# Half-step FFNs of a hybrid decoder layer: hidden blocks that `down` takes plainly without their sums, another order of the second pair's sums, and other ways for the first P6 weights, the first norm's gain and the last weights of `down`

## The chip, the cores and the metric

The kernel runs on one core of one Trainium2 chip. The metric is device time of one launch in microseconds; the time of the kernel before is the median of three runs. One further execution was taken by the hardware profiler, and every row below is from that one. In the rows PE is TensorE (matmuls and transposes; PEld its weight loads), DVE is VectorE, ACT ScalarE, POOL GpSimd, SP SyncE. SPq and ACTq are the DMA issues of SP and ACT.

## The reference

One layer of a hybrid decoder for 1040 prompt positions (16 learned tokens and 1024) and 64 sample positions: a half-step FFN, a token mixer (gated delta rule beside sliding-window attention), and a second half-step FFN. The change lies in the FFNs and in what comes just before each.

```python
def rms_norm(x, g):
    xf = x.astype(jnp.float32)
    y = xf * lax.rsqrt(jnp.mean(xf * xf, axis=-1, keepdims=True) + RMS_EPS)
    return (y * g.astype(jnp.float32)).astype(x.dtype)

def swiglu(x, w_gate, w_up, w_down):
    return (jax.nn.silu(x @ w_gate) * (x @ w_up)) @ w_down

def half_ffn(h, g_pre, g_post, w_gate, w_up, w_down):
    return h + 0.5 * rms_norm(swiglu(rms_norm(h, g_pre), w_gate, w_up, w_down), g_post)
```

`D_MODEL` is 1024, `D_FF` 2816, and all is float32.

## The kernel before, in words

Each FFN is one object of class `Ffn` (lines 168 to 577). It multiplies by one level of the Strassen-Winograd scheme: tokens (1104 in FFN1, 1088 in FFN2), model width and hidden width are each halved, and seven products P1 to P7 of half-size blocks take the place of eight. The sums and differences of token blocks are the `x1` to `x7` tiles (`left` makes x1 and x2 of a tile of 128 tokens, `right` the other five, from two tiles and with transposes on TensorE, `place`, line 206). Those of weight blocks are `T` (`difference`, line 254, on VectorE). Every operand is split into a high part, cast on ACT (`wh` line 278, `x..h` line 208, `hs` line 370) and a low part, the rest, subtracted on POOL for weights (`wl` line 279) and on VectorE otherwise (`x..l` line 209, `hs` line 358). A product is three matmuls per step, high by high, low by high, high by low (`FAST`). One product of a pair has 24 pairs of matmuls in gate and up and goes to PSUM bank A, B or C (line 305).

The hidden width is handled in 11 pairs f = 0 to 10 of 128 columns from each half. The order of a pair is gate (kind g), then up (kind u); `start` runs P1 and P2 of the first two pairs while the tokens come in (`weave` puts pieces of two generators into the program in turn, here matmuls and `tiles_in` for FFN1, `Merge.rest` for FFN2), then `ea1`, the pools of that phase, are closed, others opened, and `up(2)` runs the rest: P6, P5, P7, P4, P3 for the first two pairs and P1, P6, P5, P7, P2, P4, P3 for the others, each for g and u. The adds that take a bank away are on VectorE: `u2` after P6 (line 343), `s` after P7 and, on the same P7 plus bank C, `u3` (line 346), then after P4 and P3. P4 goes to a B bank (two of them), which the add after P6 sets free; P3 is added on top of P5 in bank C, which `u3` has read first.

When a pair is done, `hidden(f)` multiplies gate by up and makes the seven operand blocks that the products of `down` need. Blocks 1, 4, 8 and 2 are the plain ones, 5, 6, 7 and 3 are sums and differences of them, `S1` and `S2` hold them. `split` makes both parts, and `store` writes them to DRAM (`hid`) from ACT's queue, the last pair's, f = 10, mostly from SP's (line 376). It is a generator: `self.late` is advanced one step after each product of the following pair but P6, and what is left is drained at the end of `up`.

`down` goes over groups of pairs (0, 1), (2, 3, 4), (5, 6), (7, 8), (9, 10). For each of the seven products of a group it loads the blocks (`hb`, from SP's queue, line 458) and multiplies them by split weight blocks into accumulators (line 473); the first group copies its products to the accumulators on ACT (line 512), in the order P1, P2, P3, P6, P5, P7, P4. The last group, f = 9 and 10, is `plain`: it uses the four ordinary products with weights 11, 21, 12 and 22 and reads blocks 1, 2, 8 and 4 alone. Its weights lie in two pools, `wp` (that of the groups before) and `wp2`. VectorE and POOL add accumulators to one another meanwhile (`beside`).

The framework orders the instructions of each engine by its own estimate of time, and the waits between engines are semaphores; an instruction waits at the head of its engine's queue, a DMA issue as well.

## Time and profile before

| | |
|---|---|
| median of 3 runs | 2802.1 us (2795.24 to 2806.37) |
| the profiled execution's own time | 2796.77 us |
| its span | 2795.0 us |
| TensorE busy | 2669.6 us, 96% |
| VectorE, ACT, POOL busy | 1619.9, 1099.8, 1390.0 us |
| mean granted TensorE clock | 0.979 |
| DMA | 413.88 MB, 148 GB/s over the span |

FFN1 ends near 760 us, the mixer near 1950, FFN2 at the end. The chain of work that ended last is TensorE nearly all along. A wait of TensorE is a row "engine line waited for: us in total, times, longest us". In a window's row stand the stretch, its length, busy us of the engine (with the number of instructions), the granted clock (1.00 is full), the DMA engines' share and GB/s.

### The profile page before, as it was taken

To read this page: it belongs to the slowest core of one execution; us is meant where nothing else is said; L and a number is where in the kernel's file an instruction comes from. 1 tells how busy PE (TensorE), PEld (TensorE's weight loads), DVE (VectorE), ACT (ScalarE), POOL (GpSimd) and SP (SyncE) were. 2 spreads that over 40 slices of the span, in tenths; PEclk is the share of its full clock that TensorE was granted. 3 is DMA by queue.
4 is the path that set the end of the run, shared out by engine and by line. 5 is a ranking of instruction groups with operands and counts; after the bars stand their busy time and mean duration, and the time that the engine had idled before them with its cause. 6 is when DMAs were issued, how large, how long until landed. Compare 5 with 4: busy or idle time off the path is not lost. (4 is left out here: it accounts for less than half of the span.)

```text
span 2795.0 us, 49454 instructions
## 1 busy us (share of the span) xinstructions
PE 2669.6 (96%) x18957; PEld 2502.6 (90%) x18957; DVE 1619.9 (58%) x2415; ACT 1099.8 (39%) x2592; POOL 1390.0 (50%) x1296
## 2 busy tenths in 40 slices
PE   7999999899978999999999999998999999999998
PEld 6999999899977898788788888887789999999997
DVE  7757566446546659954444444443557556555575
ACT  5333333322155632354444444444443334343221
POOL 5655555445446644644434443444455555554471
PEclk9999999999988999999999999999999999999998
DMA  4344343677433653354333333334434344348763
GB/s 154 130 150 159 122 151 143 246 237 239 168 121 113 212 180 96 99 170 116 100 88 95 94 92 95 92 92 138 136 125 157 118 153 162 118 151 325 240 224 122
DMA packets 230994, 413.88 MB, mean 148 GB/s; under 512 B 59894, under 2 KB 121494, under 8 KB 230470
## 3 DMA queue, kind: packets, MB, share of 16 engines
q1 hardware_dynamic: 209302, 327.67, 36.5%
q10 hardware_dynamic: 21456, 83.05, 7.4%
q8 instruction: 150, 2.46, 0.4%
q14 instruction: 86, 0.70, 0.1%
HBM read 262.78 MB, written 149.51 MB: 148 GB/s over the span
## 5 line engine op out<-in xcount | busy, mean ns | idle before, releaser
L132 PE MATMUL gu<-xh,wl 128*128 128x512 f32 (+3 forms) x1456 | 502.8, 345 | 0.1
L279 POOL TENSOR_TENSOR wl<-T,wh 128x512 fp32r<-128x512 f32 x248 | 338.3, 1370 | 326.7 <-ACT wh L278 237.0
L128 PE MATMUL gu<-xh,wh 128*128 128x512 f32 (+3 forms) x1456 | 498.5, 342 | 0.0
L130 PE MATMUL gu<-xl,wh 128*128 128x512 f32 (+3 forms) x1456 | 497.4, 342 | 0.0
L473 PE MATMUL y<-hb,wh 128*128 128x256 f32 (+2 forms) x2528 | 434.7, 292 | 15.8 <-DMA hb<-hid 9.7
L279 POOL TENSOR_TENSOR wl<-raw,wh 128x512 fp32r<-128x512 f32 x198 | 272.5, 1382 | 267.3 <-ACT wh L278 220.5
L473 PEld LDWEIGHTS y<-hb,wh 128*128 128x128 f32 x2528 | 370.1, 190 | 18.1 <-DMA hb<-hid 10.5
L132 PEld LDWEIGHTS gu<-xh,wl 128*128 128x128 f32 x1456 | 281.6, 193 | 28.8 <-issue 11.1
L130 PEld LDWEIGHTS gu<-xl,wh 128*128 128x128 f32 x1456 | 281.9, 194 | 19.9 <-issue 1.2
L128 PEld LDWEIGHTS gu<-xh,wh 128*128 128x128 f32 x1456 | 281.8, 194 | 18.6 <-issue 1.6
L278 ACT CAST wh<-T 128x512 fp32r<-128x512 f32 x248 | 153.3, 621 | 349.0 <-PE B L305 109.0
L473 PE MATMUL y<-hb,wl 128*128 128x256 f32 (+2 forms) x1264 | 274.5, 291 | 5.5 <-POOL wl L279 5.5
L278 ACT CAST wh<-raw 128x512 fp32r<-128x512 f32 x198 | 122.1, 620 | 288.5 <-PE y L473 103.5
L484 DVE TENSOR_TENSOR acc<-acc,y 128x552 f32<-128x552 f32 (+4 forms) x216 | 144.9, 679 | 154.3 <-PE y L473 153.8
L752 POOL TENSOR_TENSOR wl<-raw,wh 128x1024 fp32r<-128x1024 f32 x60 | 145.4, 2424 | 143.5 <-ACT wh L751 121.1
L473 PEld LDWEIGHTS y<-hb,wl 128*128 128x128 f32 x1264 | 208.9, 190 | 6.8 <-POOL wl L279 6.7
L254 DVE TENSOR_TENSOR T<-raw,raw 128x512 f32<-128x512 f32 x124 | 118.7, 960 | 105.5 <-POOL wl L279 102.6
L1514 POOL TENSOR_TENSOR f<-f,mhalf 128x1 f32<-128x1 f32 (+1 forms) x72 | 54.6, 759 | 113.1 <-DVE f L1512 107.5
L264 DVE TENSOR_TENSOR T<-raw,T 128x512 f32<-128x512 f32 x62 | 70.9, 1146 | 67.9 <-POOL wl L279 67.8
L905 DVE SCALAR_TENSOR_TENSOR cv<-pc,cw,cv 128x1131 f32<-128x1131 f32 x48 | 75.1, 1567 | 34.2 <-POOL cv L902 33.8
L254 DVE TENSOR_TENSOR T<-raw,T 128x512 f32<-128x512 f32 x62 | 65.6, 1064 | 32.1 <-POOL wl L279 31.9
L370 ACT CAST hs<-S 128x552 fp32r<-128x552 f32 (+1 forms) x60 | 39.1, 652 | 111.3 <-DVE S L358 68.1
(585 smaller groups left out, 7489.0 us busy)
## 6 DMA issues: line engine op xcount, KB each, us to landing
hid<-hs ACTq DMA_DIRECT2D x73, 552.0 KB
hid<-hs ACTq DMA_DIRECT2D x73, 544.0 KB
hb<-hid SPq DMA_DIRECT2D x71, 552.0 KB
hb<-hid SPq DMA_DIRECT2D x71, 544.0 KB
raw<-in_w_in_dram SPq DMA_DIRECT2D x58, 512.0 KB
raw<-in_ffn_w_gate_dram SPq DMA_DIRECT2D x94, 256.0 KB
raw<-in_ffn_w_up_dram SPq DMA_DIRECT2D x94, 256.0 KB
raw<-in_ffn_w_down_dram SPq DMA_DIRECT2D x88, 256.0 KB
```

The source lines that it names most:

```text
L128: nc.tensor.matmul(ps, wh, xh, start=first and i == 0, stop=False)
L130: nc.tensor.matmul(ps, wh, xl, start=False, stop=False)
L132: nc.tensor.matmul(ps, wl, xh, start=False, stop=last and i == n - 1)
L254: self.nc.vector.tensor_tensor(out=b[name], in0=b[x], in1=b[y], op=ALU.subtract)
L264: nc.vector.tensor_tensor(out=s, in0=b["21"], in1=s, op=ALU.subtract)
L278: self.nc.scalar.copy(hi, s)
L279: self.nc.gpsimd.tensor_tensor(out=lo, in0=s, in1=f32(hi), op=ALU.subtract)
L473: self.nc.tensor.matmul(self.view(ps[d], (i,)), w[x][:, d * P:(d + 1) * P], hb[:, y, lo:hi], start=j + x + y == 0, stop=j == len(items) - ...
L484: dve = lambda out, x, y: nc.vector.tensor_tensor(out=out, in0=x, in1=y, op=ALU.add)
L752: nc.gpsimd.tensor_tensor(out=lo, in0=raw, in1=f32(hi), op=ALU.subtract)
L905: nc.vector.scalar_tensor_tensor(out=cv, in0=pc[:, w:w + PADW], scalar=self.cw[:, j, w:w + 1], in1=cv, op0=ALU.mult, op1=ALU.add)
L1514: nc.gpsimd.tensor_tensor(out=f[rows], in0=f[rows], in1=c.mhalf[rows, 0:1], op=ALU.pow)
```

## The change

- `hidden`: for f = 9 and 10 only blocks 1, 4, 8 and 2 are made and stored; 5, 6, 7 and 3 and the sums for them are not. That is sixteen stores fewer in the two FFNs.
- `hidden`, other pairs: blocks come in the order 1, 4, 5, 2, 6, 7, 3 (before 1, 4, 5, 6, 2, 7, 3). Both sums are made in the step of block 5, and h12 - S2 is written to S1 in the step of block 2.
- `up`: the steps of `hidden(0)` that follow P7 and P4 of pair 1's gate are issued after the add of P6.
- `sixth_ahead` (new): called before `ea1` closes, it loads blocks 11, 12 and 22 of the first pair's gate weights, makes T2 and splits it, so that the first P6's weights are made there. `w_op` makes T1 and T2 for P4 itself where they are not there.
- `down`, last group: weights 11 and 21 are split into `wp2`, 12 and 22 into `wp`.
- `tiles_in`: the first norm's gain, 1024 values that all partitions need, is loaded as one row from ACT's queue and spread by two matmuls with a row of ones and two copies on VectorE. Norms 2 and 3 are put between the steps of `left(1)`, and their operations keep program order.
- The weaves of `start` with `tiles_in` and `rest` begin at 0.25 of the matmuls (0 and 0.1 before).

```diff
+    def sixth_ahead(self):
+        b, = self.raw("g", (0,), ("11", "12", "22"))
+        t = self.c.t(self.rawp, [P, 512], tag="raw")
+        for out, x, y in ((t, b["12"], b["11"]), (b["22"], b["22"], t)):
+            self.nc.vector.tensor_tensor(out=out, in0=x, in1=y, op=ALU.subtract)
+        self.ready[0, "g", 6] = self.w_split(self.wp, b["22"])
...
             if len(parts) == 2 and p != 6:
-                next(self.late, None)
+                with self.c.tc.issue_after(self.sixth) if p in (7, 4) and (f, kind) == self.begun else nullcontext():
+                    next(self.late, None)
...
         h12 = times("u2")
+        if f in self.plain:
+            split(8, h21)
+            yield
+            store()
+            split(2, h12)
+            yield
+            store()
+            yield
+            return
         s1, s2 = self.v("S1"), self.v("S2")
         op(s1, h21, h22, ALU.add)
+        op(s2, s1, h11, ALU.subtract)
         split(5, s1)
-        yield
-        store()
-        op(s2, s1, h11, ALU.subtract)
-        split(6, s2)
         yield
         store()
         split(2, h12)
-        if f in self.plain:
-            split(8, h21)
+        op(s1, h12, s2, ALU.subtract)
+        yield
+        store()
+        split(6, s2)
+        yield
+        store()
         op(h21, h11, h21, ALU.subtract)
+        split(7, h21)
         yield
         store()
-        split(7, h21)
-        op(s2, h12, s2, ALU.subtract)
-        yield
-        store()
-        split(3, s2)
+        split(3, s1)
...
-        w = {name: [self.w_split(self.wp if name[1] == "1" else self.wp2, x[name]) for x in b]
+        w = {name: [self.w_split(self.wp2 if name[1] == "1" else self.wp, x[name]) for x in b]
...
-                    gain("ffn1_norm_pre", xin)
+                    row, one = c.t(xin, [1, D], tag="row", bufs=1), c.t(xin, [1, P], tag="one", bufs=1)
+                    nc.scalar.dma_start(row, I["ffn1_norm_pre"])
+                    nc.gpsimd.memset(one, 1.0)
+                    g = gains["ffn1_norm_pre"] = c.t(xin, [P, D], tag="g", bufs=1)
+                    for k in range(0, D, 512):
+                        ps = c.t(ptr, [P, 4, P], tag="tr").rearrange("p k t -> p (k t)")
+                        nc.tensor.matmul(ps, one, row[:, k:k + 512], start=True, stop=True)
+                        nc.vector.tensor_copy(g[:, k:k + 512], ps)
...
-                if t in order[:5]:
+                if j == 1:
+                    yield from steps_of(g := f1.left(ptr, xs[t], t), 1)
+                    next(g)
+                    norm(2, c.tc.keep_in_program_order)
+                    norm(3, c.tc.keep_in_program_order)
+                    yield
+                elif t in order[:5]:
...
-        weave((steps_of(first, 48), 0, 1, 48), (steps_of(tr, 6), 0, 0.9, 6))
+        weave((steps_of(first, 48), 0, 1, 48), (steps_of(tr, 6), 0.25, 1, 6))
```

SP's queue at the start of FFN1's `down`, before: `hid` are the stores of the last pair's blocks, `hb` the loads of `down` (the first is the second block of P3, the next two P6's, the fourth P5's), `raw` its weights.

```order
L458 DMA hb_6176<-hid_6_70 128x1104
L376 DMA hid_6_70<-hs_5934 128x1104
L458 DMA hb_6251<-hid_6_70 128x1104
L247 DMA raw_6533<-in_ffn_w_down_dram 128x512
L376 DMA hid_6_70<-hs_5939 128x1104
L376 DMA hid_6_70<-hs_5943 128x1104
L376 DMA hid_6_70<-hs_5946 128x1104
L247 DMA raw_6535<-in_ffn_w_down_dram 128x512
L376 DMA hid_6_70<-hs_5952 128x1104
L376 DMA hid_6_70<-hs_5957 128x1104
L458 DMA hb_6252<-hid_6_70 128x1104
L458 DMA hb_6319<-hid_6_70 128x1104
```

And in the changed kernel:

```order
L248 DMA raw_6505<-in_ffn_w_down_dram 128x512
L390 DMA hid_6_70<-hs_5927 128x1104
L390 DMA hid_6_70<-hs_5931 128x1104
L480 DMA hb_6150<-hid_6_70 128x1104
L480 DMA hb_6225<-hid_6_70 128x1104
L248 DMA raw_6507<-in_ffn_w_down_dram 128x512
L248 DMA raw_6509<-in_ffn_w_down_dram 128x512
L480 DMA hb_6226<-hid_6_70 128x1104
L480 DMA hb_6293<-hid_6_70 128x1104
L248 DMA raw_6511<-in_ffn_w_down_dram 128x512
L248 DMA raw_6513<-in_ffn_w_down_dram 128x512
L480 DMA hb_6294<-hid_6_70 128x1104
```

Of six stores two are left; they stand ahead of P3's `hb` now, and P6's second `hb` stands behind two loads and no store.

VectorE's queue in the second pair's gate of FFN1, before, from the third operation after the sum `S1` on (`u2g`, line 343, is the add of P6 that P4 waits for, `sg` of line 343 that of P7, `u3g`, line 346, is what P3 waits for; `hs` and `S` belong to `hidden(0)`, `T` to weights):

```order
L358 TENSOR_TENSOR hs_1121<-S_189_1118,hs_1121 128x552
L358 TENSOR_TENSOR hs_1198<-S_190_1119,hs_1198 128x552
L358 TENSOR_TENSOR hs_1236<-u2g_813,hs_1236 128x552
L358 TENSOR_TENSOR S_190_1119<-u2g_813,S_190_1119 128x552
L358 TENSOR_TENSOR hs_1273<-sg_246,hs_1273 128x552
L264 TENSOR_TENSOR T_1322<-raw_1318,T_1322 128x512
L343 TENSOR_TENSOR u2g_1165<-sg_552,B_1140 128x552
L358 TENSOR_TENSOR hs_1308<-S_190_1119,hs_1308 128x552
L254 TENSOR_TENSOR T_1540<-raw_1498,raw_1496 128x512
L343 TENSOR_TENSOR sg_552<-u2g_1165,B_1207 128x552
L358 TENSOR_TENSOR hs_1419<-g_130_669,hs_1419 128x552
L346 TENSOR_TENSOR u3g_1233<-sg_552,C_1171 128x552
```

And in the changed kernel, from the third operation after `S1` on:

```order
L372 TENSOR_TENSOR S_197_1136<-u2g_827,S_198_1137 128x552
L372 TENSOR_TENSOR hs_1216<-u2g_827,hs_1216 128x552
L266 TENSOR_TENSOR T_1340<-raw_1336,T_1340 128x512
L353 TENSOR_TENSOR u2g_1184<-sg_561,B_1159 128x552
L372 TENSOR_TENSOR hs_1255<-S_198_1137,hs_1255 128x552
L372 TENSOR_TENSOR sg_241<-g_80_312,sg_241 128x552
L255 TENSOR_TENSOR T_1559<-raw_1517,raw_1515 128x512
L372 TENSOR_TENSOR hs_1292<-sg_241,hs_1292 128x552
L353 TENSOR_TENSOR sg_561<-u2g_1184,B_1226 128x552
L372 TENSOR_TENSOR hs_1326<-S_197_1136,hs_1326 128x552
L372 TENSOR_TENSOR hs_1437<-g_134_678,hs_1437 128x552
L358 TENSOR_TENSOR u3g_1252<-sg_561,C_1190 128x552
```

The add of P6 stands six rows after `S1` where it stood nine rows after it, and the rows that it passed stand behind it: `u3g` is the fourteenth row after `S1` in both.

## Rows read from the trace of the kernel before

**Rows 1.** The page, part 1: busy us, share of the span, instructions.
```profile
PE 2669.6 (96%) x18957; PEld 2502.6 (90%) x18957; DVE 1619.9 (58%) x2415; ACT 1099.8 (39%) x2592; POOL 1390.0 (50%) x1296
```
**Rows 2.** TensorE's waits over the whole span: us in total, times, longest us.
```profile
PE tr L206 <- DVE x L90: 12.6, 3, 8.0
PE y L473 <- DMA hb<-hid: 9.7, 4, 7.4
...
PE B L305 <- DVE u2g L343: 6.4, 2, 3.3
PE y L473 <- ACT acc L512: 6.2, 3, 4.1
PE B L305 <- ACT wh L278: 5.7, 2, 3.7
PE y L473 <- POOL wl L279: 5.5, 4, 2.5
...
PE tr L206 <- DVE x41l L209: 2.1, 1, 2.1
```
**Rows 3.** TensorE windows after waits: length, busy us, granted clock, DMA share, GB/s.
```profile
64.55:69.40 4.85, 4.78 (x24) 0.66 0.55 166
109.21:113.70 4.49, 4.49 (x24) 0.66 0.86 317
544.82:551.00 6.18, 6.18 (x33) 0.65 0.80 301
...
2077.36:2082.70 5.34, 4.75 (x25) 0.68 0.34 109
2122.18:2126.80 4.62, 4.62 (x25) 0.63 1.02 373
2553.04:2558.00 4.96, 4.96 (x28) 0.68 0.87 357
2724.57:2732.00 7.43, 7.43 (x37) 0.62 0.01 2
```
**Rows 4.** Timeline at the start (VectorE, ACT), and line 1584's matmuls: ns min/median/max.
```profile
6.68 1.28 DVE L90 SCALAR_TENSOR_TENSOR x<-x,rn,g_ffn_norm_pre 128x1024 f32<-128x1024 f32 x1 [6.68 <-POOL rn L83]
...
4.58 1.06 ACT L81 ACTIVATE dump<-x 128x1024 bf16<-128x1024 f32 x1 [2.12 <-DMA x<-in_x_prompt_dram]
...
L1584 PE MATMUL on<-xe,kd x32: 589/641/694, 1408.7 to 1905.3; 64*128 64x512 f32 x32
```
**Rows 5.** Timeline of VectorE before the first P6: start us, us.
```profile
61.23 0.32 DVE L209 TENSOR_TENSOR x31l<-tr,x31h 128x160 fp32r<-128x160 f32 x1 [0.80 <-ACT x31h L208]
```
**Rows 6.** VectorE: one `hs` form (ns min/median/max), then the second pair's two adds.
```profile
L358 DVE TENSOR_TENSOR hs<-u2g,hs x22: 708/720/1824, 103.6 to 2534.3; 128x552 fp32r<-128x552 f32 x11, 128x544 fp32r<-128x544 f32 x11
...
108.34 0.72 DVE L343 TENSOR_TENSOR u2g<-sg,B 128x552 f32<-128x552 f32 x1
...
111.51 0.72 DVE L346 TENSOR_TENSOR u3g<-sg,C 128x552 f32<-128x552 f32 x1
```
**Rows 7.** Timeline of SP's queue at the start of FFN1's `down`.
```profile
526.61 0.38 SPq L458 DMA_DIRECT2D hb<-hid  x1
...
535.32 4.75 SPq L376 DMA_DIRECT2D hid<-hs  x2
540.17 1.28 SPq L458 DMA_DIRECT2D hb<-hid  x2
```
**Rows 8.** A window there: all engines, then granted clock, DMA share, GB/s.
```profile
530.00:540.00 10.00, 6.68 (x51) 6.24 (x49) 7.94 (x9) 4.05 (x7) 7.41 (x4) 1.00 0.99 385
```
**Rows 9.** Timeline of ACT at the start of FFN2's `down`.
```profile
2552.38 1.64 ACT L512 COPY acc<-y 128x544 f32<-128x544 f32 x3 [7.17 <-DMA hid<-hs]
```
**Rows 10.** Timeline of ACT at the last group of FFN1's `down`.
```profile
719.50 1.38 ACT L278 CAST wh<-raw 128x512 fp32r<-128x512 f32 x2 [4.74 <-PE y L473]
```
**Rows 11.** Timelines of VectorE and TensorE in a steady pair.
```profile
185.95 0.72 DVE L343 TENSOR_TENSOR u2g<-sg,B 128x552 f32<-128x552 f32 x1
...
189.87 0.28 PE L305 MATMUL B<-x40h,wh 128*128 128x256 f32 x1
```

More of the change, by code (lines that the diff above doesn't have):

```diff
@@ L1 @@
 import itertools
-from contextlib import ExitStack, contextmanager
+from contextlib import ExitStack, nullcontext
 import numpy as np
@@ L72, in bcast_rows, with rstd @@
     return bass.AP(tensor=ap.tensor, offset=ap.offset, ap=[[0, n]] + [list(x) for x in ap.ap])
-def rstd(c, pool, x, n, scale, eps, tag, dump=None):
+def rstd(c, pool, x, n, scale, eps, tag, dump=None, pin=lambda op: op):
     nc = c.nc
@@ L80, in rstd @@
         dump = c.t(pool, [P, D], BF16, tag="dump", bufs=1)
-    nc.scalar.activation(dump[:n], x[:n], AF.Square, accum_out=r[:n])
+    pin(nc.scalar.activation(dump[:n], x[:n], AF.Square, accum_out=r[:n]))
     nc.gpsimd.tensor_scalar(out=r[:n], in0=r[:n], scalar1=scale, scalar2=eps, op0=ALU.mult, op1=ALU.add)
@@ L84, in rstd, with normed @@
     return r
-def normed(c, pool, x, n, g, dump=None):
-    r = rstd(c, pool, x, n, 1.0 / D, EPS, "n", dump)
-    c.nc.vector.scalar_tensor_tensor(out=x[:n], in0=x[:n], scalar=r[:n, 0:1], in1=g[:n], op0=ALU.mult, op1=ALU.mult)
+def normed(c, pool, x, n, g, dump=None, pin=lambda op: op):
+    r = rstd(c, pool, x, n, 1.0 / D, EPS, "n", dump, pin)
+    pin(c.nc.vector.scalar_tensor_tensor(out=x[:n], in0=x[:n], scalar=r[:n, 0:1], in1=g[:n], op0=ALU.mult,
+                                         op1=ALU.mult))
 def pre_norm(c, pool, psum, x, out, n, g, evac):
@@ L192, in __init__ @@
         self.X = {p: [None, None] for p in range(1, 8)}
-        self.st, self.ready, self.early, self.fin, self.late = {}, {}, {}, {}, iter(())
+        self.st, self.ready, self.early, self.fin, self.late, self.begun = {}, {}, {}, {}, iter(()), None
     def x_tiles(self, pool, p, parts):
@@ L262, in w_op @@
         if p == 4:
-            s = b["T2"]
+            made("T1", "12", "11")
+            s = made("T2", "22", "T1")
             nc.vector.tensor_tensor(out=s, in0=b["21"], in1=s, op=ALU.subtract)
@@ L342, in gate_up @@
                         st[out] = self.v(out + kind)
-                    nc.vector.tensor_tensor(out=st[out], in0=st[x], in1=ps, op=ALU.add)
+                    add = nc.vector.tensor_tensor(out=st[out], in0=st[x], in1=ps, op=ALU.add)
+                    if p == 6:
+                        self.sixth = add.ins
                 if p == 7:
@@ L393, in hidden @@
         store()
-        op(s2, s1, h11, ALU.subtract)
+        split(2, h12)
+        op(s1, h12, s2, ALU.subtract)
+        yield
+        store()
         split(6, s2)
@@ L397, in hidden @@
         store()
-        split(2, h12)
-        if f in self.plain:
-            split(8, h21)
         op(h21, h11, h21, ALU.subtract)
+        split(7, h21)
         yield
         store()
-        split(7, h21)
-        op(s2, h12, s2, ALU.subtract)
-        yield
-        store()
-        split(3, s2)
+        split(3, s1)
         yield
@@ L437, in up @@
     def up(self, started):
+        self.begun = started - 1, "g"
         for f in range(NF // 2):
@@ L1878, in load, with norm @@
                 if t == 0:
-                    gain("ffn1_norm_pre", xin)
-            def norm(t):
-                normed(c, xin, xs[t], h if abs(t) == 8 else P, gains["ffn1_norm_pre"])
+                    row, one = c.t(xin, [1, D], tag="row", bufs=1), c.t(xin, [1, P], tag="one", bufs=1)
[6 more added lines that the diff above has]
+                        nc.vector.tensor_copy(g[:, k:k + 512], ps)
+            def norm(t, pin=lambda op: op):
+                normed(c, xin, xs[t], h if abs(t) == 8 else P, gains["ffn1_norm_pre"], pin=pin)
             load(0)
@@ L1897, in tiles_in @@
                         load(order[j + 2])
-                if j + 2 < len(order):
+                if 1 < j and j + 2 < len(order):
                     norm(order[j + 2])
@@ L1907, in body @@
         drain(tr)
+        f1.sixth_ahead()
         ea1.close()
@@ L1979, in body @@
         rest = mg.rest()
-        weave((steps_of(first, 48), 0, 1, 48), (steps_of(rest, 7), 0.1, 0.9, 7))
+        weave((steps_of(first, 48), 0, 1, 48), (steps_of(rest, 7), 0.25, 0.95, 7))
         weave((first, 0, 1, 49), (steps_of(rest, 5), 0.1, 0.8, 5))
         weave((f2.start(1, False), 0, 1, 49), (steps_of(rest, 5), 0.1, 0.8, 5))
+        f2.sixth_ahead()
         ea1.close()
```

## The prediction, made before the result was known

> **What bounds the kernel now.** I read the page's busy shares first: TensorE is busy for 2669.6 us, 96% of the span, so anything that shortens the run takes away a TensorE wait or gives its clock back; work taken off another engine counts only through that [rows 1]. Then the list of TensorE's waits over the whole span, to see which of them a part of the change can touch: the first norm's multiplication, the `hb` loads of `down`, the u2 add of the second pair, the first copies of `down`, the first P6 weights, low weight halves from POOL, and one transpose [rows 2]. Then windows that begin where such a wait ends, for the granted clock. It is 0.62 to 0.68 there, a mix of the two levels of 1.2 and 2.4 GHz, after TensorE had stood idle for 2 to 7 us. Work lost in a window is its length times one minus that clock, so the window after the longest `hb` wait lost 6.18 x 0.35 = 2.2 us, and the seven lose 1.6, 1.5, 2.2, 1.7, 1.7, 1.6 and 2.8 us in their order [rows 3]. A wait that goes is thus worth its length and up to this loss. The order listings then told what stands ahead of each awaited operation.
>
> The profiled execution took 2796.77 us, its span 2795.0 us; that is 5.3 us below the median of the three runs, 2802.1. Gains are worked out on the trace and taken off the median.
>
> **The start (A).** The gain's 512 KB broadcast is replaced by a 4 KB row, two matmuls and two copies, and the third tile's norm and transposes come later in the program. Before, the gain was not what was waited for: the first multiplication began at 6.68 us, released by the norm's own factor [rows 4]. Now it must wait for the row, the matmuls and the copies. How soon a row lands no row shows; it is at the latest with the first x tile, whose reader began at 4.58 [rows 4]. A float32 matmul with 512 columns takes 641 ns at full clock [rows 4], and at half clock, estimated, 1.3 us. With two of them and a copy of about 0.7 us the gain is there at 4.6 + 2.6 + 0.7 = 7.9, so 1.2 us late. Against it, of the two later waits on this multiplication (12.6 - 8.0 = 4.6 us [rows 2]) the one of the third tile, about half, goes. 2.3 - 1.2 gives **+1 us**. Ends: -2 (nothing of the waits goes and the queue behind loses a little more) and +3. The Trainium skill, "DMA: Bandwidth & Descriptors", section on the anatomy of one DMA, gives a fixed cost of about 2 us for a transfer; by it the row would land near 3 us, the gain would be ready at about the old time and A would be +2; no row here shows it.
>
> **First P6 (B).** Its weights were made after the pools switched, and TensorE waited 3.7 us for them, until 64.55 [rows 2, 3]. Now three loads, two subtractions and the split come before the switch. P6 still needs the low part of the last transposed tile, which VectorE makes at 61.23 in 0.32 [rows 5]: it can begin at 61.6, so 2.9 us go. P5's weights (T1, no longer made for P6) come out at about the old time, which I estimate to take back 0.5; half of the clock loss, 0.8, is returned. FFN1: 3.2. In FFN2 the wait is 5.7 - 3.7 = 2.0 [rows 2], plus half of 1.7: 2.8. Together **+6.0**; at worst 3 (P5 waits instead, clock stays low), at best 5.7 of waits and 3.3 of clock, 9.0. The extra T1 and T2 operations that P4 now makes itself fall on VectorE while P5 and P7 run, six microseconds of cover.
>
> **P4 of the second pair (C).** TensorE waits twice for the u2g add, 6.4 us in all [rows 2]. In the new order three fewer VectorE operations stand between the pair-0 sums and this add, and each takes 0.72 us or, when POOL works, 1.8 [rows 6]: it can come 2.2 to 5 us earlier and P4's wait goes. But P3 accumulates into the C bank and needs the u3g add, and ahead of that the order has as many operations as before. It began at 111.51 [rows 6] and ended 112.2. P4 was released at 109.21 after 3.1 us and ran 4.49, of which 1.5 are clock loss [rows 2, 3]; without its wait it goes from 106.1 to 109.1, and P3, which began at 113.7, can begin at 112.2 after 3 us of idling, but then loses the 1.5 of the clock itself: 112.2 + 1.5 = 113.7. **0 us**: the wait moves from P4 to P3. Ends: -3 (u3g a microsecond or two later in both FFNs) and +6 (it comes as early as u2g).
>
> **Start of down (D).** SP's queue is in order. In FFN1 one `hb` load of P3 went at 526.61, then came the stores of the last pair, two of them not before 535.32, and behind these the second `hb` of P6 at 540.17, which released TensorE at 544.82 [rows 7, 3]. Six stores before that load become two, since the plain group reads only four of the eight blocks, and the waits of VectorE for store buffers go with the other four. The two that stay now stand ahead of P3's `hb`, which comes perhaps a microsecond later: -1.1. P6's second `hb` goes near 530, as I estimate from the two weight loads that still stand ahead of it, and lands, as before after 4.6 us, near 535; P3 ended at 544.8 - 7.4 = 537.4 and will at 538.5. So 7.4 [rows 2] + 2.0 of the 2.2 clock loss - 1.1 = 8.3. If the two stores are late by 3 us more, 5. The stretch before has the DMA engines at 0.99 and 385 GB/s [rows 8]. If bytes and not the order of the queue made the load late, the four stores of 0.56 MB less give 2.2 MB / 385 GB/s = 5.9 us instead of 7.4, and D1 is 6.8. The Trainium skill, "DMA: Bandwidth & Descriptors", section "Issuing engines are not separate DMA queues", says that transfers from any engine share the same 16 engines, so only bytes would count. I keep the queue's reading, since the load was issued no earlier than 540.17 and landed 4.6 us later even then. In FFN2 ACT's copies of `down` into new accumulators stood 7.17 us until stores had read their buffers [rows 9], and TensorE 4.1 for the copies [rows 2]; those last stores are gone. 4.1 + half of 1.6 = 5. D together **+13.3** (8 to 15).
>
> **Last group of down (E).** Weights 11 and 21 came from buffers that the preceding group still used: ACT's cast was held 4.74 us by TensorE [rows 10], POOL's low halves behind it cost TensorE 5.5 us in four waits [rows 2] and 2.8 of clock in FFN2 [rows 3]. Now they come from the other pool, idle then; 12 and 22 take the late one and are read only when the blocks of 11 and 21 are through, four times 24 matmuls, some 12 us. 5.5 + 2.8 = **+8.3**; if POOL stays the brake, 4.5.
>
> **Weave in FFN2 (F).** The transposes that waited 2.1 us for x41l [rows 2] come about ten matmuls later: 2.1, and a little of a clock loss that I put at 1.7, like the windows of the other waits of 2 us: **+2.5** (0 to 3.8).
>
> **The order of hidden for all other pairs (G).** Per pair it is the same number of operations in another order. In steady pairs the u2g add began at 185.95, P4 at 189.87 [rows 11]: with 0.72 for the add, 3.2 us of slack, and nine operations stand ahead of the add, before as now. **0**. The stores left out (sixteen, 9 MB) and 34 fewer VectorE operations lie beside TensorE's work otherwise: 0.
>
> Sum: 1 + 6.0 + 0 + 13.3 + 8.3 + 2.5 + 0 = 31.1. So 2802.1 - 31.1 = **2771 us**. Lower ends: -2 + 3 - 3 + 8 + 4.5 + 0 = 10.5. Upper: 3 + 9.0 + 6 + 15 + 8.3 + 3.8 = 45.1.
>
> **Rivals.** *The waits move on.* P3, P5 and the two stores ahead of P3's `hb` take over, clock losses stay: the lower ends together, 2791.6 us, inside 0.5%. For it: C, where I expect just this; against it: D and E each have a direct releaser that is gone. *All goes*: the upper ends, 2757; for it: the waits are short chains, against it: C. *Slower*: one mechanism, the new order of `hidden` in the steady pairs, 18 in all. If the u2g or u3g add came later than the 3.2 us slack, each excess microsecond would cost 18 us; from 2.5 us of excess, 5.7 us later in all, it costs 45 us, eats the 31 and gives 2816. For it: VectorE operations grow from 0.72 to 1.8 us where POOL works [rows 6], and a reorder changes which are hit; against it: that needs five more such hits per pair, with equal counts. *E not as said* (the other pool's buffers are no earlier): 8 us less, 2779, still faster; it is part of the forecast's spread.
>
> **How the numbers follow.** Half a percent, 14 us, is about what a measurement of this kernel tells from none. Chances: forecast with its spread 0.70, all goes 0.08, waits move on 0.17, slower 0.05; so faster 0.78, same 0.17, slower 0.05. The range runs from the upper ends, less the 5 us by which the median may sit off, to the lower ends: 2752 to 2792.
>
> **What would show it.** In the list of waits: no TensorE wait on `hb` over 2 us, none on wl L279 of `down`, a wait of P3 for u3g in place of P4 for u2g, P6 starting near 61.6 us; the first transposes near 9 us; steady pairs without a gap. A wait of over 0.5 us in each pair, a first norm after 10 us, or an unmoved `hb` wait near 537 would make me wrong.

## The result, and the profile after

The changed kernel takes **2786.5 us** (median of 5, 2782.66 to 2790.69). The kernel before, run beside it, took 2802.1 (median of 5, 2795.24 to 2807.26); the ratio is 0.995, 95% interval 0.9934 to 0.9965. It is faster by 15.6 us (9.8 to 18.5 by the interval), half of the 31.1 forecast. The profiled execution took 2782.66 us, its span 2780.8, which is 14.1 and 14.2 less than the profiled one of before; all that follows is worked out on these two.

The page's busy shares, columns as in [rows 1]: VectorE lost 34 operations, TensorE's idle time is 117.1 us of the span where it was 125.4.
```profile
PE 2663.7 (96%) x18961; PEld 2495.5 (90%) x18961; DVE 1586.3 (57%) x2381; ACT 1096.9 (39%) x2584; POOL 1389.3 (50%) x1297
```
TensorE's waits over the whole span, to be read against [rows 2] (the lines have moved: `y` is now L495, the split L280 and L281, `u2` L353 and `u3` L358):
```profile
PE C L315 <- DVE u3g L358: 10.9, 4, 4.2
...
PE y L495 <- DMA hb<-hid: 7.3, 5, 4.3
...
PE A L315 <- ACT x11h L209: 3.7, 2, 2.6
...
PE tr L207 <- POOL x L229: 2.5, 2, 1.7
...
PE tr L207 <- DVE x L229: 1.3, 1, 1.3
PE y L495 <- ACT acc L534: 1.3, 2, 1.0
...
PE tr L207 <- DVE sum L229: 1.1, 1, 1.1
...
PE B L315 <- DVE u2g L353: 1.1, 2, 0.5
PE B L315 <- DVE x31l L210: 0.7, 1, 0.7
```
No row on `wh` or `wl` is left, and u2g went from 6.4 to 1.1: what the change aimed at is gone. In its place stand u3g (10.9), the tiles' own sums on VectorE and POOL (`x` and `sum` of L229), `x11h`, and another `hb` (7.3 in all, 4.3 of it in one wait). Windows of TensorE, columns as in [rows 3]: the second pair's P3 in FFN1, P3's second half in `down`, and, in FFN2, P6, the second pair's P3, the first copies of `down` and its last group.
```profile
119.10:124.29 5.19, 5.19 (x24) 0.56 0.43 159
541.38:546.00 4.62, 4.62 (x20) 0.50 0.99 373
2075.29:2078.29 3.00, 3.00 (x26) 1.00 0.79 273
2123.79:2128.41 4.62, 4.62 (x25) 0.63 0.39 161
2554.00:2558.00 4.00, 4.00 (x34) 1.00 0.66 264
2724.00:2732.00 8.00, 8.00 (x67) 1.00 0.03 4
```
FFN2's P6, its first copies and its last group have their full clock (0.68, 0.68 and 0.62 in [rows 3]); the two P3 and the new `hb` wait do not.

So that every part has its share, the span was cut at the starts of TensorE's products, read from the two timelines:

| stretch of TensorE | before | after | gained |
|---|---|---|---|
| FFN1: start to first P6 | 64.55 | 68.01 | -3.5 |
| first P6 to first P3 | 14.02 | 15.42 | -1.4 |
| first P3 to P6 of the second pair's up | 38.18 | 40.86 | -2.7 |
| to the first matmul of `down` | 399.12 | 399.13 | 0 |
| `down`, matmuls 1 to 400 | 62.78 | 58.46 | +4.3 |
| 400 to 1400; 1400 to 1700; rest | 127.33; 41.03; 32.02 | 127.55; 39.03; 32.68 | -0.2; +2.0; -0.7 |
| mixer, to FFN2's first P1 | 1260.02 | 1255.66 | +4.4 |
| FFN2: first P1 to first P6 | 38.31 | 38.49 | -0.2 |
| first P6 to first P3 | 14.32 | 13.35 | +1.0 |
| first P3 to P6 of the second pair's up | 38.12 | 39.77 | -1.7 |
| to the first matmul of `down` | 393.48 | 393.48 | 0 |
| `down`, 1 to 400 | 57.18 | 51.07 | +6.1 |
| 400 to 1400; 1400 to 1700; rest | 124.45; 43.94; 46.15 | 124.44; 37.34; 46.06 | 0; +6.6; +0.1 |

The mixer's code is the same in both. Over the runs below it took 1253.8 to 1263.5 us, 1255.6 in one with before's code, so its 4.4 are no gain of the change: on this pair of executions the change itself gave 9.8. (By these stretches FFN1's `down` ends at 779.0 us before, and FFN2's first P1 begins at 2039.1; the times near 760 and 1950 given with the profile before are too early.)

### The profile page after: what moved, and what is told of

It reads as the page before. It is cut to its first block, busy times and chain, and to the rows that moved or that the text cites. A ratio compares the mean times of both kernels' runs of the same rounds, so it can differ in the third digit from the quotient of the medians.

```text
span 2780.8 us, 49379 instructions
## 1 busy us (share of the span) xinstructions
PE 2663.7 (96%) x18961; PEld 2495.5 (90%) x18961; DVE 1586.3 (57%) x2381; ACT 1096.9 (39%) x2584; POOL 1389.3 (50%) x1297
## 5 line engine op out<-in xcount | busy, mean ns | idle before, releaser
L281 POOL TENSOR_TENSOR wl<-T,wh 128x512 fp32r<-128x512 f32 x246 | 330.5, 1349 | 345.1 <-ACT wh L280 254.4
L495 PE MATMUL y<-hb,wh 128*128 128x256 f32 (+2 forms) x2528 | 432.2, 291 | 8.5 <-DMA hb<-hid 7.3
L281 POOL TENSOR_TENSOR wl<-raw,wh 128x512 fp32r<-128x512 f32 x200 | 281.5, 1414 | 248.8 <-ACT wh L280 198.8
L495 PEld LDWEIGHTS y<-hb,wh 128*128 128x128 f32 x2528 | 367.6, 189 | 10.4 <-DMA hb<-hid 7.9
L280 ACT CAST wh<-T 128x512 fp32r<-128x512 f32 x246 | 152.4, 620 | 377.5 <-PE B L315 117.0
L495 PE MATMUL y<-hb,wl 128*128 128x256 f32 (+2 forms) x1264 | 272.4, 289 | 0.0
L280 ACT CAST wh<-raw 128x512 fp32r<-128x512 f32 x200 | 122.2, 620 | 286.4 <-PE C L315 87.8
L495 PEld LDWEIGHTS y<-hb,wl 128*128 128x128 f32 x1264 | 208.0, 189 | 0.0
L1067 DVE TENSOR_TENSOR la<-la,ltmp 72x14 f32<-72x14 f32 (+37 forms) x76 | 80.1, 1054 | 1.3
```

Of the source, the lines that this page charges most:

```text
L280: self.nc.scalar.copy(hi, s)
L281: self.nc.gpsimd.tensor_tensor(out=lo, in0=s, in1=f32(hi), op=ALU.subtract)
L495: self.nc.tensor.matmul(self.view(ps[d], (i,)), w[x][:, d * P:(d + 1) * P], hb[:, y, lo:hi], start=j + x + y == 0, stop=j == len(items) - ...
L1067: nc.vector.tensor_tensor(out=a[:n, 0:j, j + 1:size], in0=a[:n, 0:j, j + 1:size], in1=t, op=ALU.add)
```

## The experiments

Theory after the result: TensorE's waits were called right where a direct releaser was named, and three things were not seen, the order of the tiles' work on VectorE and POOL at the start (A), u3g's rows (C), and two stores ahead of P3's `hb` (D). Rival: each new wait is the price of one part (the row for the gain, the pinned norms, the weave) and would be there without the others. Where nothing else is said, an experiment is the changed kernel with one part put back, and one execution was profiled; runs of the same code differ by 5 us and more through the mixer alone, so the verdicts go by stretches of the table.

**The start, four parts put back one at a time.**

```diff
 e1_weaves
-        weave((steps_of(first, 48), 0, 1, 48), (steps_of(tr, 6), 0.25, 1, 6))
+        weave((steps_of(first, 48), 0, 1, 48), (steps_of(tr, 6), 0, 0.9, 6))
-        weave((steps_of(first, 48), 0, 1, 48), (steps_of(rest, 7), 0.25, 0.95, 7))
+        weave((steps_of(first, 48), 0, 1, 48), (steps_of(rest, 7), 0.1, 0.9, 7))
 e2_gain
-                    row, one = c.t(xin, [1, D], ...
...
+                    gain("ffn1_norm_pre", xin)
 e5_norms
-                if j == 1:
...
-                elif t in order[:5]:
+                if t in order[:5]:
 e3_no_sixth
-        f1.sixth_ahead()
-        f2.sixth_ahead()
```

> The changed kernel with the two weaves at the fractions of before (0 to 0.9 in FFN1, 0.1 to 0.9 in FFN2); the rest as changed. In the changed kernel the first P6 begins at 68.0 us, 3.5 us later than before, although its weights no longer hold it: the last token tile is late. Theory W (the transposes, put later among the matmuls, make the whole chain of token tiles late): the first P6 begins 4 to 6 us earlier, at 62 to 64 us. Theory G (the gain by row makes the first transposes 2.8 us late, at 10.8 us, and everything after them): P6 moves by less than 1 us, 67 to 68. Theory S (the loads and subtractions made ahead for P6 stand in the chain of the tiles): also less than 1 us. FFN2's first P6, relative to the first product of FFN2: W says 2 to 3 us earlier.

> The changed kernel with the gain by the 512 KB broadcast of before. Theory G: first transposes at about 8 us (10.8 changed), first P6 at 65 to 66 us (68.0 changed). Theory W: the start gains at most 1 us at the first P6, 67 to 68, since the later tiles are late for another reason.

> The changed kernel with the norms of tiles 2 and 3 where they stood before and without their program order. Theory N (the fixed place of these norms puts the later tiles back): first P6 2 us or more earlier, at most 66 us. Theories W, G and S: 67 to 69 us.

> The changed kernel without the P6 weights made ahead. Theory S (its loads, two subtractions, cast and low part stand in the chain of token tiles): the last token tile is done 2 us or more earlier than in the changed kernel (67.7 us), but P6 then waits for its weights, some 3 us as before, so P6 begins at 68 to 70 us. Theory W: the last tile is done within 0.5 us of 67.7 and P6 begins at 70 to 71 us. Both: the wait of P3 of the first pair for its u3g add (1.4 us in FFN1, 1.2 in FFN2) goes, if the T2 that P4 now makes itself is its cause.

| | whole, us (before, run beside the four: 2805.52) | first transposes | first P6 of FFN1 | FFN2, P1 to P6 |
|---|---|---|---|---|
| changed kernel (beside another before, 2802.1) | 2782.66 | 10.82 | 68.01 | 38.49 |
| e1_weaves | 2777.75 | 10.77 | 62.88 | 36.26 |
| e2_gain | 2785.95 | 8.13 | 63.76 | 41.79 |
| e5_norms | 2786.13 | 11.56 | 61.30 | 40.77 |
| e3_no_sixth | 2789.54 | 10.82 | 66.34, of it 3.7 a wait for `wh` | 41.44 |

Three more kernels below have the very start of the changed one, with P6 at 67.82, 68.56 and 68.82, and two runs with the start of e5_norms are 1.4 us apart (below); a difference of 2 us and more is one. Put back alone, the weaves, the gain and the norms each let P6 begin 4 to 7 us sooner; in e3_no_sixth P6 itself begins only 1.7 sooner, since it waits for its weights again, but the low part of the last tile, `x31l`, which P6 needs too, is made 4.6 us sooner (at 63.02 after 67.63). They can't cost that much each, since the sum would be over 20 us, and the whole loss is 6.9 (against e13_oldstart below); so they cost it together, and each theory that gave the loss to one part alone falls. The norms' old place is enough by itself: e5_norms keeps the other three parts and begins P6 at 61.30, where e13_oldstart with the whole old start begins it at 61.16. In FFN2 the weave is what shows: with the new one P1 to P6 took 38.06 to 41.79 in the eight kernels here that have the changed code there, with the old one 36.1 to 36.8 in three.

**Where the time is lost.** VectorE of the changed kernel around tile 6's norm, columns as in [rows 4]:
```profile
42.57 2.11 DVE L90 SCALAR_TENSOR_TENSOR x<-x,rn,g 128x1024 f32<-128x1024 f32 x1
44.60 0.68 DVE L210 TENSOR_TENSOR x60l<-tr,x60h 128x512 fp32r<-128x512 f32 x1
45.20 0.68 DVE L210 TENSOR_TENSOR x30l<-tr,x30h 128x512 fp32r<-128x512 f32 x1
45.80 0.45 DVE L347 TENSOR_TENSOR g<-g,C 128x296 f32<-128x296 f32 x1
46.17 0.68 DVE L299 TENSOR_TENSOR raw<-raw,raw 128x512 f32<-128x512 f32 x1
46.77 0.68 DVE L229 TENSOR_TENSOR sum<-x 128x512 f32<-128x512 f32 x1
...
58.54 1.28 DVE L90 SCALAR_TENSOR_TENSOR x<-x,rn,g 40x1024 f32<-40x1024 f32 x1
```
And its POOL:
```profile
49.98 2.23 POOL L281 TENSOR_TENSOR wl<-raw,wh 128x512 fp32r<-128x512 f32 x1 [2.71 <-ACT wh L280]
52.16 2.98 POOL L229 TENSOR_TENSOR x<-sum,x 128x512 f32<-128x512 f32 x2
```
Between the norm and tile 6's `sum`, which that tile's transposes wait for (1.1 us in the list of waits), stand four operations, one of them the first subtraction for the weights made ahead (L299); on POOL the low part of these weights, which waited 2.71 us for its cast, stands ahead of the tiles' `x`. In e5_norms:
```profile
39.09 1.27 DVE L90 SCALAR_TENSOR_TENSOR x<-x,rn,g 128x1024 f32<-128x1024 f32 x1
...
41.49 0.68 DVE L229 TENSOR_TENSOR sum<-x 128x512 f32<-128x512 f32 x1
...
43.66 0.68 DVE L299 TENSOR_TENSOR raw<-raw,raw 128x512 f32<-128x512 f32 x1
```
Here, as in e1_weaves and e2_gain, `sum` is 2.4 us behind the norm and the subtraction follows it; in the changed kernel it is 4.2, of which 0.8 is the norm itself, 2.11 us where it took 1.27. This is one piece of the loss: against e13_oldstart the changed kernel is 2.8 us late when tile 6's norm begins (39.75 there), 4.6 at its `sum` (42.14), 5.8 at the last tile's norm (52.72) and 6.9 at P6. Two runs took this reading on. e11_pin ties four low parts of the tile before behind tile 6's norm; e15_behind ties the weights made ahead behind the tiles' sums (the two subtractions, the cast and the low part, FFN1 only; `mark` holds the last tile's `sum` and its last `x` on POOL).

```diff
 e11_pin
-            self.place(psum, p, i, o, src, n)
+            with self.c.tc.issue_after(self.c.normed.ins) if self is self.c.f1 and t == 5 and p in (5, 7, 6, 3) else nullcontext():
+                self.place(psum, p, i, o, src, n)
 e15_behind
-        op(nc.vector, s, y1, y2, ALU.add)
+        self.mark = [op(nc.vector, s, y1, y2, ALU.add)]
...
-        op(nc.gpsimd, x2, x2, x1, ALU.subtract)
+        self.mark.append(op(nc.gpsimd, x2, x2, x1, ALU.subtract))
...
-            self.nc.vector.tensor_tensor(out=out, in0=x, in1=y, op=ALU.subtract)
-        self.ready[0, "g", 6] = self.w_split(self.wp, b["22"])
+            with self.c.tc.issue_after(self.mark[0].ins) if self is self.c.f1 else nullcontext():
+                self.nc.vector.tensor_tensor(out=out, in0=x, in1=y, op=ALU.subtract)
+        with self.c.tc.issue_after(self.mark[1].ins) if self is self.c.f1 else nullcontext():
+            self.ready[0, "g", 6] = self.w_split(self.wp, b["22"])
```

> The changed kernel with the four low parts of token tile 5 put behind the norm of tile 6 on VectorE, so that this norm stands two rows earlier (its sum stays where it was, behind them); nothing else moves. In the changed kernel that norm began at 42.6 us (39.4 before) and the first P6 at 68.0. If these two rows are what makes the later tiles late: first P6 at 62 to 65 us. Rival (each lap of the chain load, norm, sums, transposes loses a little on ACT, SP and TensorE as well, and no single row decides): norm 1 us earlier, P6 at 66 to 68.

> The changed kernel, with the four operations that make the first P6 weights ahead issued later in FFN1: the two subtractions on VectorE behind the last tile's sum, the cast on ACT and the low part on POOL behind the last tile's last sum there. Nothing else is moved by hand. Theory that the weights made ahead stand in the token tiles' way (the subtraction ahead of tile 6's sum on VectorE, the low part ahead of tile 6's operations on POOL): sum of tile 6 within 3 us of its norm instead of 4.5, last tile's norm near 55 instead of 58.5, the first P6 at 62 to 64 instead of 68.01, the whole 4 to 6 us under the changed kernel. Rival, that these operations only fill gaps there and the delay comes from the tiles' own order (norms 2 and 3 and the weave): sum still 4 us or more behind its norm, P6 at 67 or later, or P6 now waiting on its own weights. The waits of the second pair and of down stay as in the changed kernel by both.

e11_pin (2790.77 us, before 2800.03): P6 at 67.41, the norm at 42.31, `sum` at 46.87: the rival held, the norm's place alone decides nothing. e15_behind (2783.34, before 2803.79): P6 at 65.93, 1.9 to 2.9 us sooner than in the four runs of the changed start (50.1 us after its own first P1, 52.1 to 53.2 there), and POOL is no longer among TensorE's waits there. VectorE of e15_behind:
```profile
42.46 2.10 DVE L90 SCALAR_TENSOR_TENSOR x<-x,rn,g 128x1024 f32<-128x1024 f32 x1
...
46.06 0.68 DVE L229 TENSOR_TENSOR sum<-x 128x512 f32<-128x512 f32 x1
...
57.32 1.28 DVE L90 SCALAR_TENSOR_TENSOR x<-x,rn,g 40x1024 f32<-40x1024 f32 x1
...
59.72 0.68 DVE L300 TENSOR_TENSOR raw<-raw,raw 128x512 f32<-128x512 f32 x1
...
61.52 0.68 DVE L300 TENSOR_TENSOR raw<-raw,raw 128x512 f32<-128x512 f32 x1
```
62 to 64 was expected, so it is between the two theories: the weights made ahead stand in the tiles' way, and moving them back is worth 2 to 3 of the 7 us. It need not be all that they cost: the moved subtractions now stand between the last tile's own operations (59.72, 61.52), and `x31l`, at 65.55 here, is at 63.02 in e3_no_sixth, which has none of them. The other operations that stand between norm and `sum` when all parts are together (`x60l`, `x30l`, `g`) were not moved in a run that helped. How the rest of the loss divides among them stays open.

**The second pair's sums.** e4_old_sums has the old order of `hidden` and no late issue; e7_cfix keeps the new order and issues the late steps behind the add for u3 in place of the one of P6.

```diff
 e4_old_sums
-        op(s2, s1, h11, ALU.subtract)
         split(5, s1)
         yield
         store()
+        op(s2, s1, h11, ALU.subtract)
+        split(6, s2)
+        yield
+        store()
         split(2, h12)
...
-                with self.c.tc.issue_after(self.sixth) if p in (7, 4) and (f, kind) == self.begun else nullcontext():
-                    next(self.late, None)
+                next(self.late, None)
 e7_cfix
-                    nc.vector.tensor_tensor(out=st["u3"], in0=st["s"], in1=self.view(st["C"], parts), op=ALU.add)
+                    self.third = nc.vector.tensor_tensor(out=st["u3"], in0=st["s"], in1=self.view(st["C"], parts),
+                                                         op=ALU.add).ins
...
-                with self.c.tc.issue_after(self.sixth) if p in (7, 4) and (f, kind) == self.begun else nullcontext():
+                with self.c.tc.issue_after(self.third) if p in (7, 4) and (f, kind) == self.begun else nullcontext():
```

> The changed kernel with the sums of before in their old order and no step put behind the P6 add. The stretch from P3 of the first pair to P6 of the second pair's up kind took 38.19 us before and 40.86 changed (FFN1), 38.11 and 39.76 (FFN2). If the new order and the pinned steps are the cause: 38.2 and 38.1 again, within 0.3, with TensorE waiting at P4 for u2g and not at P3. Rival (the later phase of the pool engine's low halves after the new start, not the order): 39.5 to 41 still. The steady pairs from there to the first product of down took 399.1 and 393.5 us in both kernels and stay.

> The changed kernel with the two steps put behind the u3 add instead of behind the P6 add, so that five fewer operations stand ahead of u3g on VectorE. If P3 waits for the number of operations ahead of u3g: its wait of 4.2 us falls to 0 to 1.5 us, its product runs at full clock, and the stretch of 40.86 us (FFN1) becomes 35 to 37, 39.76 (FFN2) 34 to 36. Rival (the operations put off come back as a wait in the up kind of the same pair, or at the end of hidden): the stretch to the first product of down grows by what is won, 399.1 to 402 or more.

Both ran beside a before of 2800.84 us. e4_old_sums: 2783.29, first P3 to the up's P6 39.67 in FFN1 and 38.01 in FFN2 (changed kernel 40.86 and 39.77). e7_cfix: 2779.59, 37.27 and 35.66. Waits in e4_old_sums:
```profile
PE B L315 <- DVE u2g L353: 6.4, 2, 3.3
...
PE C L315 <- DVE u3g L358: 2.6, 2, 1.4
```
and in e7_cfix:
```profile
PE C L315 <- DVE u3g L358: 6.0, 4, 2.1
...
PE B L315 <- DVE u2g L353: 1.1, 2, 0.6
```
The new order with the changed kernel's place for the late steps is 1.2 and 1.8 us worse than the old one; behind u3 it is 2.4 and 2.4 us better. Over the eight runs here with the changed code for these sums the stretch took 40.1 to 42.6 and 39.7 to 40.7; the old order lies under that (in FFN1 only just), and e7_cfix well under it. The steady stretch to `down` stays at 399.24 and 393.65, so nothing comes back as a wait there.

Two of the expected ranges were missed. e7_cfix's 37.27 is over 35 to 37, since the first pair's P3 loses clock there (last section). e4_old_sums came back to before's 38.1 in FFN2 but not to 38.2 in FFN1; 39.67 lies in the rival's range. Its wait at P4 for u2g is that of before (3.04 us, 3.06 before) and the second pair's P3 waits no more, as expected; P4 then ran at a lower clock, 5.66 us here and 4.49 at 0.66 before ([rows 3]), which is 1.2 of the 1.5:
```profile
113.95:119.61 5.66, 5.66 (x25) 0.50 0.68 259
```
So the order of the sums accounts for where TensorE waits; why the clock stayed low for longer no run shows.

**The start of `down`.** e9_hb_act loads P3's `hb` of the first group from ACT's queue; e10_plain is the kernel before with nothing changed but the plain pairs' blocks and the pools of the last weights (D and E alone).

```diff
 e9_hb_act
-    def values(self, hbp, group, p):
+    def values(self, hbp, group, p, queue=None):
...
-            self.nc.sync.dma_start(f32(x), self.h_d[f, p - 1].rearrange("p (x t) -> p x t", x=2))
+            (queue or self.nc.sync).dma_start(f32(x), self.h_d[f, p - 1].rearrange("p (x t) -> p x t", x=2))
...
-                items = list(zip(w, got.pop(p, None) or self.values(hbp, group, p)))
+                items = list(zip(w, got.pop(p, None) or self.values(hbp, group, p, nc.scalar if vi == 0 and p == 3 else None)))
 e10_plain, against the kernel before
         h12 = times("u2")
+        if f in self.plain:
+            split(8, h21)
...
+            return
...
-        w = {name: [self.w_split(self.wp if name[1] == "1" else self.wp2, x[name]) for x in b]
+        w = {name: [self.w_split(self.wp2 if name[1] == "1" else self.wp, x[name]) for x in b]
```

> The changed kernel with the two blocks of P3 in the first group of down loaded from ACT's queue. In the changed kernel TensorE waits 4.3 us for the second of them, which stands behind the two stores and fourteen weight loads on SP. If the place in SP's queue is the cause: wait 0 to 1 us, and the first 400 matmuls of FFN1's down take 52.5 to 54.5 us instead of 58.5 (62.8 before); FFN2's stay at 51.1. Rival (the transfer itself, with the DMA engines at 0.6 to 0.8 of their time, is late, or ACT is held up by the load and its copies take its place): 57 to 59.

> The kernel before with only the plain pairs' blocks left out and the last group's weights in the other pool. If these two parts alone make down shorter: the first 400 matmuls of down take 58 to 59 us in FFN1 and 51 in FFN2 (62.8 and 57.2 before), the last group's wait for low halves goes (stretch of matmuls 1400 to 1700: 39 and 37.3 instead of 41.0 and 44.0), the start and the second pair stay as before (first P6 at 64.6, stretch 38.2), and the whole is some 16 to 18 us shorter than before, which is as much as the whole change. Rival (down gains only with the later start or the new order of the sums): less than 10 us.

e9_hb_act: matmuls 1 to 400 of FFN1's `down` take 52.80 us where the changed kernel takes 58.46; in FFN2 51.92 (51.07). The whole was 2789.31 with a mixer of 1263.5. ACT's queue there, the two loads, and the waits of TensorE between 520 and 580:
```profile
510.20 0.35 ACTq L480 DMA_DIRECT2D hb<-hid  x1
...
530.94 0.33 ACTq L480 DMA_DIRECT2D hb<-hid  x1
```
```profile
PE y L495 <- DMA hb<-hid: 1.1, 1, 1.1
```
The same bytes by another queue: the second load was issued 5.5 us after the first matmul of `down`, 12.3 in the changed kernel, and P3 no longer waits (the 1.1 is at a later product). So the load's place in SP's queue made P3 wait. The busy DMA engines had a part in it that this run doesn't separate: from issue to release the changed kernel's load took 5.70 us, 4.41 before, and in that time the engines were at 1.01 of their time (0.83 before):
```profile
535.68:541.38 5.70, 1.38 (x12) 0.89 1.01 373
```
e10_plain: 2775.51 us where the one run of before beside it took 2800.84; matmuls 1 to 400 58.39 and 51.36, 1400 to 1700 39.07 and 37.67, start and second pair as before (P6 at 63.99, 38.30). The 25.3 us between the two are over the 16 to 18 expected, but 4.5 of them are the mixer, and the before that was profiled was itself 4 us faster. By stretches D and E alone give 4.4 + 5.8 + 2.0 + 6.3 = 18.5 us, less 2.0 in matmuls 400 to 1400 (128.22 and 125.56), which is 16.5: more than the 9.8 of the whole change, so its other parts together cost time.

**Versions that beat both.** e12_best is the changed kernel with the edits of e5_norms, e7_cfix and e9_hb_act and of FFN2's weave alone; e13_oldstart has those of e2_gain and FFN1's weave as well, so FFN1's whole old start, with the weights made ahead kept.

> The changed kernel with what the runs so far say: norms 2 and 3 where they stood before, FFN2's weave at the old fractions, the two steps of the second pair behind the u3 add, P3's blocks in the first group of down from ACT's queue. If the stages add up: first P6 of FFN1 at 61 to 63 us (-5 to -7 against the changed kernel), second pair -3.5 in each FFN, start of FFN1's down -5.5, FFN2's start -2: some 19 us less than the changed kernel, 2767 us, ratio to before 0.987 to 0.990. Rival (a gain at the start shifts the phase of the clock or of the queues and is lost behind, as the changed kernel's own parts were): 2775 to 2782, ratio 0.991 to 0.994.

> As the run before it, but with the whole start of FFN1 as before the change (gain by the broadcast, norms and weaves as before) and the P6 weights still made ahead. If the new start is worth nothing by itself: within 2 us of the run before it, first P6 at 61 to 63 us. If the row gain and the late third tile are worth what I forecast for them: 1 us slower than that run or more.

e12_best: 2766.1 us (4 runs, 2760.42 to 2768.21), 0.9875 of before (0.986 to 0.9889). e13_oldstart: 2765.2 (5 runs, 2759.92 to 2769.76), 0.9874 (0.9859 to 0.989), before 2800.03. They are equal, 20 us under the changed kernel. P6 begins at 62.66 and 61.16, first P3 to the up's P6 takes 35.72 and 35.68, and 37.21 and 35.66, matmuls 1 to 400 of `down` 52.5 to 53.0 and 52.0 to 52.8, FFN2's P1 to P6 36.78 and 36.11. The gain by row and FFN1's later weave, which e12_best still has, are thus worth nothing of themselves. (Up to P6, FFN1's start is the same in e12_best and e5_norms, 62.66 and 61.30: so far apart can two runs of one start be.)

## Where the prediction failed and where it held

| term | predicted | measured | from |
|---|---|---|---|
| A start of FFN1 | +1 | -6.9 | e13_oldstart's P6 at 61.16 against 68.01 |
| B first P6 | +6.0 | +4.9 | 64.55 - 61.16 - 1.4; 38.31 - 36.4 + 1.0 |
| C second pair | 0 | -4.3 | table |
| D start of `down` | +13.3 | +10.4 | table |
| E last group | +8.3 | +7.8 | table, matmuls 400 to the end, both FFNs |
| F weave of FFN2 | +2.5 | -2.1 | 36.4 (old weave, three runs) to 38.49 |
| G steady pairs | 0 | 0 | table |

The sum is 9.8 against 31.1, and 4.4 came from the mixer, whose code is the same: that the measured time lies as near the forecast as it does is in part luck. Of the signs that the prediction named, a steady stretch without a gap, no wait for `wl` in `down`, and P3 waiting for u3g in P4's place came true; no `hb` wait over 2 us (it was 4.3) and P6 near 61.6 (68.01) did not.

**A is the step that failed.** Its +1 was 2.3, half of the norm's later waits, less 1.2 for a gain that comes late: it priced the waits for one multiplication and took the queues behind it for unchanged. It measured -6.9. The row itself went as worked out, though longer:
```profile
4.79 3.75 PE L1907 MATMUL tr<-row,one 1*128 1x512 f32 x4 [4.79 <-DMA row<-in_ffn_norm_pre_dram]
10.82 1.97 PE L207 MATMUL tr<-ident,x 128*128 128x128 f32 x8 [2.28 <-DVE x L90]
```
It landed at 4.79, where 4.6 was the bound. The Trainium skill's fixed cost of about 2 us ("DMA: Bandwidth & Descriptors", the section on the anatomy of one DMA, which is on transfers issued from GpSimd; this one went from ACT's queue) would have had it near 3, and the trace does not agree. Matmuls and copies took 4.7 more where 3.3 were put down, and the transposes began at 10.82 instead of 8.02. Only 0.85 of that reached the first P1 (14.82 after 13.97; it began at 15.7 to 16.1 in five other runs with this start). The other 6.0 were lost between P1 and the first P6. TensorE there, in the changed kernel and in e13_oldstart:
```profile
14.82:68.01 53.19, 43.03 (x316) 0.94 0.30 95
```
```profile
13.95:61.16 47.21, 41.89 (x317) 1.00 0.33 111
```
It idles 10.2 us against 5.3 and is busy 1.1 us longer, at the lower clock. The waits for `x` and `sum` of L229 make 5.0 of the idle time, 0.4 in e13_oldstart, which is nearly all of the difference; the others about balance. What had to be read there was the order of VectorE and POOL, not the one wait; the prediction read the order only in the second pair, at `down` and in the steady pairs. Which operations in that order cost the time is shown for the weights made ahead, 2 to 3 us, and open for the rest.

**B held.** P6 no longer waits for weights, only 0.7 for `x31l`, and e13_oldstart begins it 3.4 us sooner (2.9 predicted). What takes some back is not P5 but the first pair's P3, which now waits 1.43 us for u3g, as T1 and T2 for P4 are made in between; in e3_no_sixth that stretch, P5 to P3, is 9.14 and 9.00 again, as before.

**C: the mechanism was right, the size was off.** The wait moved from P4 to P3. But fourteen rows are not the same time. VectorE, the first of them and u3g, changed kernel:
```profile
103.66 1.18 DVE L372 TENSOR_TENSOR S<-sg,u3g 128x552 f32<-128x552 f32 x1
...
110.75 0.72 DVE L353 TENSOR_TENSOR u2g<-sg,B 128x552 f32<-128x552 f32 x1
...
112.04 1.82 DVE L372 TENSOR_TENSOR sg<-g,sg 128x552 f32<-128x552 f32 x1
...
118.23 0.72 DVE L358 TENSOR_TENSOR u3g<-sg,C 128x552 f32<-128x552 f32 x1
```
and the first of them in the kernel before, whose u3g is in [rows 6]:
```profile
98.75 1.18 DVE L358 TENSOR_TENSOR S<-sg,u3g 128x552 f32<-128x552 f32 x1
```
14.57 us now, 12.76 before. u2g came 2.5 us sooner (7.09 after `S`, 9.59 before), near the least of the 2.2 to 5 predicted. P3 waits 4.2 instead of 3 us and then runs at 0.56 for 5.19 us, a loss of 2.3 instead of 1.5. That the wait is for what stands ahead of u3g, e7_cfix showed. The lower end, -3, was too near.

**D: 4.0 short in FFN1, by one term.** P6's long wait is gone, but the two stores stayed late, for they stand behind `raw` loads that wait for their buffers (13.5 us in four waits for the operations `T` of VectorE that read them):
```profile
510.09 23.73 SPq L248 DMA_DIRECT2D raw<-in_ffn_w_down_dram  x14
534.13 1.45 SPq L390 DMA_DIRECT2D hid<-hs  x2
535.68 0.99 SPq L480 DMA_DIRECT2D hb<-hid  x2
```
P3's second `hb` went at 535.68 and released TensorE at 541.38, a wait of 4.33 us (0.74 before) and a window at 0.50, which lost 2.3 more: some 5.9 us, where -1.1 was put down for "perhaps a microsecond later". Counted from the first matmul of `down` it was issued 1.5 us later than before, and it took 1.3 longer to land. The prediction had named this case ("if the two stores are late by 3 us more, 5") and not given it the forecast. That the queue counts was right: e9_hb_act got 5.7 us by the queue alone. The Trainium skill, "DMA: Bandwidth & Descriptors", section "Issuing engines are not separate DMA queues", says that transfers from any engine run on the same 16 DMA engines, which no run here tests. But an issue that waits holds back what is behind it in its own engine's queue (the 14 `raw` loads above: 23.73 us), and that was the term here. FFN2's half of D gave 6.1 (5 predicted): ACT's copies no longer stand for stores.

**E and G held**: 1400 to 1700 take 39.03 and 37.34, without a wait for `wl`. In the steady pairs u2g and P4, as in [rows 11]:
```profile
192.64 0.72 DVE L353 TENSOR_TENSOR u2g<-sg,B 128x552 f32<-128x552 f32 x1
```
```profile
197.42 0.28 PE L315 MATMUL B<-x40h,wh 128*128 128x256 f32 x1
```
4.8 us apart (3.9 before): more slack than there was, and 18 pairs cost nothing; the slower rival is out.

**F went the other way.** The later transposes did shorten the wait for `x41l` (2.1 to 1.2), but TensorE then stood 2.6 us for `x11h`, which it never does in the runs with the old weave. Over the eight runs with the new one the loss was 1.7 to 5.4 us. The prediction priced the wait that a move ends and not the one it makes.

## What to carry to other kernels

A wait that a change ends is only worth its length if the next operation on that path is not late by nearly as much: list, for each engine that the moved work runs on, what now stands ahead of the next awaited operation, in microseconds and not in rows. Where a framework orders the queues by its own estimate, changes that are harmless one by one can cost time together: three of the four at the start could each be put back for 4 to 7 us, and the two parts that only took work away (D and E) gave more alone than the whole change. An engine whose queue also carries loads that wait for buffers is the wrong one for a load that TensorE needs next.

## What the runs showed that was not expected

- Four float32 matmuls for the row took 3.75 us at the start, about 0.9 each, under the 1.3 that was estimated for half clock from 641 ns [rows 4]; but it was four, not two.
- The length of the last wait does not tell what clock follows. The first pair's P3 ran 3.13 us at 1.00 after a wait of 1.43 us in the changed kernel, and 4.64 us at 0.63, 1.7 lost, after one of 2.12 in e7_cfix, whose second pair's P3 waited 1.1 and ran at 1.00. But the changed kernel's first P6 ran at 0.64 after a wait of only 0.74, and P4 of the second pair at 0.66 before and at 0.50 in e4_old_sums after the same wait of 3 us. The loss is to be read from the window. The two P3 of e7_cfix, and P6 of the changed kernel:
```profile
83.50:88.14 4.64, 4.64 (x25) 0.63 0.29 78
117.64:120.76 3.12, 3.12 (x25) 1.00 0.44 181
```
```profile
68.01:72.70 4.69, 4.69 (x25) 0.64 0.62 208
```
- The mixer, with the same code, took 1253.8 to 1263.5 us over 14 kernels, and FFN2's first stretch 38.1 to 41.8 over eight: differences of a few microseconds of the whole say little unless they are read by stretches.
